# Encoder block on one core: the gated product in its own tile, partial sums in u, w_down's work tied to rounds, two score units in the projection

## The chip, the core and the metric

The kernel runs on one core of a Trainium2 chip, as one program with one launch. The metric is the device time of that core in microseconds (us). Five engines work side by side, each through its own queue in order: PE (TensorE, matmuls and transposes; its weight loads are listed as PEld), DVE (VectorE), ACT (ScalarE), POOL (GpSimd) and SP (SyncE, which here only issues DMAs). They meet through semaphores. The profile also gives the clock that TensorE was granted, as a share of 2.4 GHz.

## What is computed

One layer of a bidirectional encoder over 1024 tokens of width 1024, in float32:

```python
h = rmsnorm(x, norm_mix_pre)                      # 1. token mixing
y = parallel_mixer(h, ...)                        #    conv group and 8-head attention, one projection in, one out
x = x + rmsnorm(y, norm_mix_post)
h = rmsnorm(x, norm_mem_pre)                      # 2. cross-attention into 256 memory tokens
y = memory_cross_attention(h, mem_n, ...)
x = x + rmsnorm(y, norm_mem_post)
h = rmsnorm(x, norm_ffn_pre)                      # 3. gated MLP, D_FF = 2816
u = dwconv_centred(h @ w_up, ffn_dw, ffn_dw_b)    #    width 3 over tokens
gate, val = u[..., :D_FF], u[..., D_FF:]
y = (gelu(gate, approximate=True) * val) @ w_down
x = x + rmsnorm(y, norm_ffn_post)
```

In the attention, query heads are normalised, rotated by position and multiplied with the keys; softmax runs over all 1024 keys.

## The kernel before, in words

Each float32 product is made of three matmuls (`gemm3`, `gemm3_multi`): operands are split into a rounded part and a remainder, both in float32r. The rounded part is a cast on ACT, the remainder a subtraction on DVE or POOL (`a_split`, L774 to L776).

The program order is not what runs: the Tile framework's scheduler works through the code with a time model of its own and fixes one order for each engine, and a tile from a pool is given out only when an earlier holder of a slot is done. Pools that matter here: `tmp` (4 slots of 128x1024), `raw` (3 slots of that size, where weights land), `W` (7 slots, the split operands), `A` (15 slots), and in PSUM `psB` (4 banks) and `psS` (2 pairs of banks). `tc.issue_after(ins)` puts the instructions of a block behind `ins` in the order of its engine.

**Projection and attention.** A loop of 16 steps (L504) projects keys and values of 8 token tiles, then queries of 8 tiles (`q_proj`, 24 matmuls each, with normalisation and rotation in a `tmp` tile, `qbuf`). Three steps behind, `q_transpose` turns a query tile into the operand `Q`. Tiles 5, 6 and 7 are turned inside the attention loop (L592, at u = 2, 4, 6). That loop runs over 64 units: `att_scores(u)` is four matmuls into a `psS` pair, a maximum on DVE (L539) and an exponential on ACT (L542) into a `tmp` tile `P`; three units later `att_transpose` turns P on PE and splits it, and every second unit `att_values` multiplies with V.

**The up stage of the MLP.** w_up is handled in 22 rounds of 128 gate and 128 value columns. A round uses a two-by-two scheme with seven products (Strassen's, in a form with shared sums) on halves of the inner and the token dimension. One product is 12 matmuls, so a round is 84. `up_first(fi)` makes the first two products (operands b11 and b21), `up_operands(fi)` the sums and splits of the weights (POOL L808 to L811, ACT L775, DVE L776), `up_finish(fi)` the products p6, p5, p3, p7 and p4 with operands t2, t1, b22, t3 and t4. The five operands of the tokens are made once, by `cross_operands` at t = 4 to 7; the last is t4, whose remainder is the last DVE step there (L708).

Partial sums go into a `tmp` tile `q`, results into a `W` tile `u` (gate and value). `conv3` is the width-3 convolution: an ACT step (L825) and two DVE steps (L826, L828). Then come the GELU on ACT (L854) and the gated product on DVE (L859), which writes into u's second half; a DMA stores this half to `act_d` (L860).

**w_down's sums, made beside.** The down stage needs four differences of w_down's blocks. For each of 22 slices `down_load` brings 512 KB into one of two halves of the `A` tile `wd_b`, `down_sums` makes four subtractions in place on DVE (L769), and `down_store` writes them to `T_d`. Nothing ties a slice to a round: only the two halves of wd_b and the order that the scheduler gave limit how soon they run. All loads and stores of the stage are issued by SP, in order.

**The down stage** (L890 on) reads act_d, w_down and T_d; its matmuls write `yd`. It runs seven products (m1, m2, m6, ...); T_d is first read by the third. Its activations land in `acts`, tiles from pool `A`.

Of the kernel before, what the change touches and what calls it, by code (L numbers as in the profile page):

```python
# [34 lines left out]
def encoder_block(ctx: ExitStack, tc: tile.TileContext, x, xT, mem, w_a, w_q, w_kv, w_mkv, w_mqT,  # L35
# [446 lines left out]
    def q_proj(t):  # L482
        pq = psB("pq")
        proj(pq, t, wq, 2)
        buf = bufs[8 + t] = tmp("qbuf")
        q3, rb = norm_rope(pq, 8, t, buf, gq[:, :128], 0.125)
        nc.vector.tensor_tensor(out=q3, in0=q3, in1=rb, op=ALU.mult)
# [12 lines left out]

    B_LAG = 3
    KV_LAG = 6
    nkv = [0]
    for i in range(16):  # L504
        if i < 16:
            (kv_proj if i < 8 else q_proj)(i % 8)
        if i >= 8:
            conv_stats(i - 8)
        if i == 13:
            conv_apply(0)  # L510
        upto = min(i - KV_LAG, 7) if i < 8 else min(7, 7 - KV_LAG + 2 * (i - 7))
        while nkv[0] <= upto:
            kv_transpose(nkv[0])
            nkv[0] += 1
        if i >= 8 + B_LAG:
            q_transpose(i - 8 - B_LAG)
    b_ctx.__exit__(None, None, None)
# [9 lines left out]
    def att_scores(u):  # L527
# [14 lines left out]
        return nc.scalar.activation(out=P, in_=sp, func=AF.Exp, bias=nm, accum_out=att_r[qp, i][:, hd:hd + 1])  # L542

# [60 lines left out]

# [21 lines left out]

    def load_raw(src, name):
        r = raw(name)
        nc.sync.dma_start(out=r, in_=src)
        return r  # L630
# [132 lines left out]
    def down_load(fi):  # L763
        nc.sync.dma_start(out=wd_b[:, fi % 2], in_=down_slice(w_down, fi))

    def down_sums(fi):
        b11, b12, b22, b21 = [wd_b[:, fi % 2, b, :] for b in range(4)]
        for dst, in0, in1 in ((b11, b12, b11), (b12, b22, b12), (b22, b22, b11), (b21, b22, b21)):
            nc.vector.tensor_tensor(out=dst, in0=in0, in1=in1, op=ALU.subtract)  # L769

    def down_store(fi):
        nc.sync.dma_start(out=down_slice(T_d, fi), in_=wd_b[:, fi % 2])

    def a_split(dst, src, eng):  # L774
        nc.scalar.copy(out=dst[:, 0, :], in_=src)  # L775
        eng.tensor_tensor(out=dst[:, 1, :], in0=src, in1=f(dst[:, 0, :]), op=ALU.subtract)  # L776
# [11 lines left out]
    def up_first(fi):  # L788
# [6 lines left out]
        q = tmp("q")  # L795
# [7 lines left out]
    def up_operands(fi):  # L803
# [12 lines left out]
        a_split(a3[:, 1], s34[:, H0], nc.vector)  # L816
# [3 lines left out]
        ups[fi] = (a2, a3, a22[0][:, fi % 2], u, q)  # L820

# [10 lines left out]
    def up_finish(fi):  # L832
        a2, a3, a22_, u, q = ups.pop(fi)

        def add(dst, ps, other, op=ALU.add, swap=False):
            nc.vector.tensor_tensor(out=dst, in0=other if swap else ps, in1=ps if swap else other, op=op)  # L836
# [14 lines left out]
        add(q[:, H0], p7, q[:, H0])  # L851
        add(u[:, 1, H1], p5, q[:, H0])
        cg = conv3(fi, 0, u)
# [5 lines left out]
        nc.vector.tensor_tensor(out=u[:, 1], in0=u[:, 0], in1=cv, op=ALU.mult)  # L859
        nc.sync.dma_start(out=act_d[fi], in_=u[:, 1])  # L860
# [11 lines left out]
    for fi in range(NF + 1):  # L872
        if fi < NF:
            if fi >= UP_PRE:
                up_first(fi)
            up_operands(fi)
        if fi == 0:
            down_load(0)
        else:
            down_store(fi - 1)  # L880
            up_finish(fi - 1)
        if fi < NF:
            down_sums(fi)
        if fi + 1 < NF:
            down_load(fi + 1)
# [208 lines left out]
```

## Time and profile before

| | us |
|---|---|
| median of 3 runs | 1452.29 (1451.33 to 1456.73) |
| the profiled execution, its own time | 1453.6 |
| its span, first to last instruction | 1451.5 |
| PE busy | 1383.5 (95%) |
| DVE busy | 1070.8 (74%) |
| ACT busy | 699.9 (48%) |
| POOL busy | 514.0 (35%) |

PE is busy for 95% of the span, so the time that any change can win lies mostly in the stretches where PE is idle or has a lower clock. Busy shares are averages over stages: the views by stretch say where PE waits, and the lists of waits say for whom. Of an engine that works in order, the instruction that waits need not be the one that matters; those behind it wait too.

### The profile page before, as it was taken

What the parts mean: (1) busy time and instruction counts of PE and PEld (TensorE: products, weight loads), DVE (VectorE), ACT (ScalarE), POOL (GpSimd) and SP (SyncE); (2) the same over time, 40 slices, a digit from 0 to 9 for tenths busy, and PEclk for the clock granted to TensorE, in tenths of its full rate; (3) what the DMA queues carried; (4) which work ended last, traced back from release to release, by engine and by line L of the source; (5) the groups of instructions that cost most, each with busy time, mean ns of one, the idle gap of its engine ahead of it and who ended that gap; (6) DMA issues with size and microseconds to landing.
All of it is one profiled execution on the core that took longest, in us unless ns stands there. A gap on an engine that the chain in (4) does not pass through costs nothing.

```text
span 1451.5 us, 18836 instructions
## 1 busy us (share of the span) xinstructions
PE 1383.5 (95%) x7042; PEld 1167.5 (80%) x7042; DVE 1070.8 (74%) x1442; ACT 699.9 (48%) x1191; POOL 514.0 (35%) x506
## 2 busy tenths in 40 slices
PE   9999999799999999999996989789999999999996
PEld 7889988679898888888885767678888888888885
DVE  6699899799998334335458878877777778985576
ACT  7426543588888434334444424234444443544452
POOL 5548887600102324002136525345554441000003
PEclk9999999999999999999998999899999999999998
DMA  6417750000000434013223576742222228622325
GB/s 236 135 59 238 243 200 14 19 1 2 30 1 12 163 103 151 24 43 131 87 87 102 174 232 198 236 135 83 74 93 81 88 87 317 226 88 88 109 87 210
DMA packets 74060, 170.08 MB, mean 117 GB/s; under 512 B 9713, under 2 KB 32497, under 8 KB 73969
## 3 DMA queue, kind: packets, MB, share of 16 engines
q1 hardware_dynamic: 73968, 168.88, 35.1%
q8 instruction: 55, 0.90, 0.3%
q14 instruction: 37, 0.30, 0.1%
HBM read 124.82 MB, written 44.04 MB: 116 GB/s over the span
## 4 chain that ended last, share of the span: by engine, by line
PE 62%; DVE 7%; DMA 5%; ACT 2%; issue 2%; POOL 1%; POOLq 0%; DVEq 0%; ACTq 0%; SPq 0%
PE p L98 7%; PE p L99 6%; PE p L101 6%; PE yd L91 5%; PE yd L92 5%; PE yd L93 5%; PE y L99 4%; PE y L101 4%; PE y L98 4%; PE pPT L82 3%; DVE wd L769 3%; DMA wd<-in_w_down_dram 2%; DMA T_d<-wd 2%; PE sc L101 2%; PE sc L98 2%; PE sc L99 2%
## 5 line engine op out<-in xcount | busy, mean ns | idle before, releaser
L305 DVE SCALAR_TENSOR_TENSOR cacc<-conv,col,cacc 128x1009 f32<-128x1009 f32 (+14 forms) x120 | 145.8, 1276 | 4.7 <-ACT cacc L253 4.5
L86 POOL TENSOR_SCALAR rt<-ss 128x1 f32<-128x1 f32 (+1 forms) x43 | 15.0, 349 | 353.5 <-DVE ss L920 227.2
L92 PE MATMUL yd<-op 128*128 128x512 f32 x308 | 119.8, 389 | 0.0
L93 PE MATMUL yd<-op 128*128 128x512 f32 x308 | 119.7, 389 | 0.0
L775 ACT CAST a<-s 128x512 fp32r<-128x512 f32 x88 | 50.8, 621 | 105.6 <-PE p L101 65.1
L91 PE MATMUL yd<-op 128*128 128x512 f32 x308 | 96.9, 389 | 0.0
L930 ACT CAST op<-acts 128x512 fp32r<-128x512 f32 x77 | 48.0, 624 | 99.6 <-PE yd L93 87.8
L776 POOL TENSOR_TENSOR a<-wg,a 128x512 fp32r<-128x512 f32 x44 | 63.1, 1456 | 84.1 <-ACT a L775 84.0
L920 DVE TENSOR_TENSOR op<-acts,op 128x512 fp32r<-128x512 f32 x77 | 53.1, 690 | 46.5 <-ACT op L930 46.4
L826 DVE SCALAR_TENSOR_TENSOR c<-u,col,c 128x1023 f32<-128x1023 f32 x44 | 56.6, 1285 | 39.9 <-ACT c L825 39.9
L557 DVE TENSOR_TENSOR PL<-pPT,PH 128x512 fp32r<-128x512 f32 x128 | 83.2, 681 | 2.4 <-ACT PH L556 1.4
L539 DVE TENSOR_REDUCE nm<-sp 128x1 f32<-128x1024 f32 x64 | 78.0, 1218 | 7.3 <-PE sp L537 6.8
L825 ACT ACTIVATE c<-u,col 128x1024 f32<-128x1024 f32 x44 | 53.2, 1209 | 54.8 <-DVE u L836 53.4
L542 ACT ACTIVATE P<-sp,nm 128x1024 f32<-128x1024 f32 x64 | 72.2, 1128 | 15.4 <-PE pPT L82 6.5
L776 DVE TENSOR_TENSOR a<-s,a 128x512 fp32r<-128x512 f32 x88 | 67.0, 779 | 15.2 <-ACT a L775 15.0
L556 ACT CAST PH<-pPT 128x512 fp32r<-128x512 f32 x128 | 69.4, 593 | 13.9 <-PE pPT L82 13.4
L769 DVE TENSOR_TENSOR wd<-wd 128x256 f32<-128x256 f32 x88 | 57.0, 664 | 20.5 <-DMA wd<-in_w_down_dram 20.0
L82 PE MATMUL pPT<-ident,P 128*128 128x128 f32 x512 | 67.9, 273 | 0.7 <-DVE PL L557 0.7
L92 PEld LDWEIGHTS yd<-op 128*128 128x128 f32 x308 | 57.8, 188 | 12.4 <-DVE op L920 0.4
L91 PEld LDWEIGHTS yd<-op 128*128 128x128 f32 x308 | 57.8, 188 | 12.0
L93 PEld LDWEIGHTS yd<-op 128*128 128x128 f32 x308 | 57.8, 188 | 12.0
L776 POOL TENSOR_TENSOR a<-wv,a 128x512 fp32r<-128x512 f32 x22 | 32.9, 1513 | 97.5 <-ACT a L775 83.1
(344 smaller groups left out, 4395.1 us busy)
## 6 DMA issues: line engine op xcount, KB each, us to landing
wg<-in_w_up_dram SPq DMA_DIRECT2D x22, 512.0 KB, 4.4
wv<-in_w_up_dram SPq DMA_DIRECT2D x22, 512.0 KB, 4.2
wd<-in_w_down_dram SPq DMA_DIRECT2D x22, 512.0 KB, 4.2
T_d<-wd SPq DMA_DIRECT2D x22, 512.0 KB, 3.9
act_d<-u SPq DMA_DIRECT2D x22, 512.0 KB, 2.9
acts<-act_d SPq DMA_DIRECT2D x22, 512.0 KB, 6.8
st<-T_d SPq DMA_DIRECT2D x20, 512.0 KB, 3.7
wmkv_r<-in_w_mkv_dram SPq DMA_DIRECT2D x16, 512.0 KB, 4.1
```

The costliest lines, as they stand in the source:

```text
L82: nc.tensor.transpose(out=out_, in_=in_, identity=ident)
L91: nc.tensor.matmul(out=ps, lhsT=sh, rhs=mh, start=first, stop=False)
L92: nc.tensor.matmul(out=ps, lhsT=sh, rhs=ml, start=False, stop=False)
L93: nc.tensor.matmul(out=ps, lhsT=sl, rhs=mh, start=False, stop=last)
L98: nc.tensor.matmul(out=p, lhsT=sh, rhs=mh, start=first, stop=False)
L99: nc.tensor.matmul(out=p, lhsT=sh, rhs=ml, start=False, stop=False)
L101: ins = nc.tensor.matmul(out=p, lhsT=sl, rhs=mh, start=False, stop=last)
L305: nc.vector.scalar_tensor_tensor(out=acc[:, t0:t1_], in0=a[:, t0 + o:t1_ + o], scalar=cc(C_DW + c * 31 + j), in1=acc[:, t0:t1_], op0=ALU.m ...
L539: nc.vector.reduce_max(out=nm, in_=sp, axis=AX.X, negate=True)
L557: nc.vector.tensor_tensor(out=PL[dst], in0=p3, in1=f(PH[dst]), op=ALU.subtract)
L769: nc.vector.tensor_tensor(out=dst, in0=in0, in1=in1, op=ALU.subtract)
L776: eng.tensor_tensor(out=dst[:, 1, :], in0=src, in1=f(dst[:, 0, :]), op=ALU.subtract)
```

## The change

Four things are changed, all in the order and the place of the work; the arithmetic is the same.

1. In the up stage the partial sums `q` move from a tmp tile into the second half of `u`, and the gated product goes to a tmp tile `o`, from which it is stored.
2. w_down's slices are tied to rounds: the load and the store of a slice stand behind the round's last w_up load in SP's order, the four subtractions of slice fi + 1 behind the seventh sum of round fi (slice 0: behind the last split of round 0).
3. Query tiles 5 and 6 take staging tiles (`raw`) in place of tmp tiles; tiles 5 to 7 are turned at u = 2, 3, 4.
4. The score units 0 and 1 are traced in the last two steps of the projection.

```diff
-        buf = bufs[8 + t] = tmp("qbuf")
+        buf = bufs[8 + t] = (raw if t in (5, 6) else tmp)("qbuf")
...
+    EARLY = 2
...
+        if i >= 16 - EARLY:
+            att_scores(i - 16 + EARLY)
...
-    for u in range(NU + LOOKAHEAD + 2):
-        if u < NU:
+    for u in range(EARLY, NU + LOOKAHEAD + 2):
+        if EARLY <= u < NU:
             ex = att_scores(u)
...
-        if u in (2, 4, 6):
-            q_transpose(8 - B_LAG + u // 2 - 1)
+        if u < EARLY + 3:
+            q_transpose(8 - B_LAG + u - EARLY)
...
     def load_raw(src, name):
         r = raw(name)
-        nc.sync.dma_start(out=r, in_=src)
+        last_load[0] = nc.sync.dma_start(out=r, in_=src)
...
     def down_load(fi):
-        nc.sync.dma_start(out=wd_b[:, fi % 2], in_=down_slice(w_down, fi))
-
-    def down_sums(fi):
+        with tc.issue_after(last_load[0].ins):
+            nc.sync.dma_start(out=wd_b[:, fi % 2], in_=down_slice(w_down, fi))
+
+    def down_sums(fi, behind):
...
+        with tc.issue_after(behind.ins):
+            for dst, in0, in1 in ((b11, b12, b11), (b12, b22, b12), (b22, b22, b11), (b21, b22, b21)):
+                nc.vector.tensor_tensor(out=dst, in0=in0, in1=in1, op=ALU.subtract)
...
     def down_store(fi):
-        nc.sync.dma_start(out=down_slice(T_d, fi), in_=wd_b[:, fi % 2])
+        with tc.issue_after(last_load[0].ins):
+            nc.sync.dma_start(out=down_slice(T_d, fi), in_=wd_b[:, fi % 2])
...
-        q = tmp("q")
+        q = u[:, 1, :]
...
-        add(q[:, H0], p7, q[:, H0])
+        seventh = add(q[:, H0], p7, q[:, H0])
         add(u[:, 1, H1], p5, q[:, H0])
+        if fi + 1 < NF:
+            down_sums(fi + 1, seventh)
...
-        nc.vector.tensor_tensor(out=u[:, 1], in0=u[:, 0], in1=cv, op=ALU.mult)
-        nc.sync.dma_start(out=act_d[fi], in_=u[:, 1])
+        o = tmp("o")
+        nc.vector.tensor_tensor(out=o, in0=u[:, 0], in1=cv, op=ALU.mult)
+        nc.sync.dma_start(out=act_d[fi], in_=o)
...
             if fi >= UP_PRE:
                 up_first(fi)
-            up_operands(fi)
-        if fi == 0:
-            down_load(0)
+                down_store(fi - 2)
+            lo = up_operands(fi)
+            down_load(fi)
+        if fi:
+            up_finish(fi - 1)
         else:
-            down_store(fi - 1)
-            up_finish(fi - 1)
-        if fi < NF:
-            down_sums(fi)
-        if fi + 1 < NF:
-            down_load(fi + 1)
+            down_sums(0, lo)
+    for fi in (NF - 2, NF - 1):
+        down_store(fi)
```

Three places show how the scheduler's order moves.

The first is PE near the end of the projection (pln and plnT are transposes of the conv group, pqT those of a query tile, sp a score unit); minus is before, plus is now.

```order
 L82 MATMUL plnT<-ident,n_2322 128x128 x8
 L82 MATMUL pln<-ident,conv_414 128x128
-L82 MATMUL pln<-ident,conv_413 128x128 x2
-L82 MATMUL pln<-ident,conv_414 128x128 x2
+L518 MATMUL sp<-KH,Q_1901 128x512
+L519 MATMUL sp<-KL,Q_1901 128x512
+L518 MATMUL sp<-KH,Q_1901 128x512
+L519 MATMUL sp<-KL,Q_1901 128x512
 L82 MATMUL plnT<-ident,n_2322 128x128 x4
 L82 MATMUL pqT<-ident,qbuf 128x128 x4
```

Score unit 0 now stands ahead of the last two query projections; the transposes of the last conv tile went behind them. Unit 1 still follows the projection.

The second is DVE at the start of the up stage, right behind t4's remainder (a<-s is a remainder of weight sums, wd<-wd one of w_down's subtractions, the other rows add a product p to a partial sum). Before:

```order
L708 TENSOR_TENSOR t4l<-r_b_6641,t4h 128x4x128 x4
L776 TENSOR_TENSOR a_7463<-s_7457,a_7463 128x512
L776 TENSOR_TENSOR a_7464<-s_7458,a_7464 128x512 x2
L776 TENSOR_TENSOR a_7490<-s_7484,a_7490 128x512
L769 TENSOR_TENSOR wd<-wd 128x256 x6
L836 TENSOR_TENSOR q<-p_7503,q 128x512
```

Now:

```order
L713 TENSOR_TENSOR t4l<-r_b_6641,t4h 128x4x128 x4
L784 TENSOR_TENSOR a_7487<-s_7481,a_7487 128x512 x2
L784 TENSOR_TENSOR a_7488<-s_7482,a_7488 128x512 x2
L845 TENSOR_TENSOR u<-p_7500,u 128x512
L776 TENSOR_TENSOR wd<-wd 128x256
L845 TENSOR_TENSOR u<-p_7501,u 128x512
```

Round 0's weight remainders went ahead of t4's, round 1's stand where they stood, and one w_down subtraction in place of six is between them and the second product's sum.

The third is a round, on DVE and on SP. DVE before, in round 2 (a_7782 belongs to round 3; c<-u,col,c is a step of the convolution):

```order
L769 TENSOR_TENSOR wd<-wd 128x256
L776 TENSOR_TENSOR a_7782<-s_7776,a_7782 128x512
L769 TENSOR_TENSOR wd<-wd 128x256
L776 TENSOR_TENSOR a_7782<-s_7776,a_7782 128x512
L769 TENSOR_TENSOR wd<-wd 128x256 x2
L836 TENSOR_TENSOR u<-p_7822,q 128x512
L769 TENSOR_TENSOR wd<-wd 128x256 x4
L826 SCALAR_TENSOR_TENSOR c<-u,col,c 128x1023
```

The same round now, from its third sum on:

```order
L845 TENSOR_TENSOR u<-p_7819,u 128x512
L835 SCALAR_TENSOR_TENSOR c<-u,col,c 128x1023
L845 TENSOR_TENSOR u<-p_7833,u 128x512
L776 TENSOR_TENSOR wd<-wd 128x256
L837 SCALAR_TENSOR_TENSOR c<-u,col,c 128x1023
L845 TENSOR_TENSOR u<-p_7792,u 128x512
L776 TENSOR_TENSOR wd<-wd 128x256
L845 TENSOR_TENSOR u<-u,p_7857 128x512
L776 TENSOR_TENSOR wd<-wd 128x256 x2
L835 SCALAR_TENSOR_TENSOR c<-u,col,c 128x1023
```

Eight subtractions in this stretch became four, all behind the seventh product's sum, and none stands ahead of a weight remainder. SP's queue in the same rounds before:

```order
L772 DMA T_d<-wd 512x1x256 x2
L764 DMA wd<-in_w_down_dram 128x4x256 x2
L772 DMA T_d<-wd 512x1x256
L629 DMA wv<-in_w_up_dram 128x1024
L764 DMA wd<-in_w_down_dram 128x4x256
L860 DMA act_d<-u 128x1024
L772 DMA T_d<-wd 512x1x256
L764 DMA wd<-in_w_down_dram 128x4x256
```

Now, one round's worth:

```order
L634 DMA wv<-in_w_up_dram 128x1024
L770 DMA wd<-in_w_down_dram 128x4x256
L634 DMA wg<-in_w_up_dram 128x1024
L780 DMA T_d<-wd 512x1x256
L872 DMA act_d<-o 128x1024
```

Where up to three slices a round went through, there is now one load and one store of w_down in each round, in a fixed cycle with the loads of w_up and the store of the gated product.

## Rows read from the trace of the kernel before

**Rows 1.** Busy time by engine, granted clock, DMA share, in stretches of the up stage.
```profile
core 0: us, PE busy (x) PEld busy (x) DVE busy (x) ACT busy (x) POOL busy (x), PEclk, DMA share, GB/s
757.96:798.90 40.94, 27.99 (x107) 21.81 (x106) 34.73 (x42) 21.14 (x39) 26.62 (x19) 0.83 0.28 90
...
803.67:980.00 176.33, 154.42 (x635) 122.77 (x636) 145.57 (x204) 61.76 (x86) 72.10 (x54) 0.94 0.60 194
980.00:1200.00 220.00, 220.00 (x972) 182.21 (x972) 159.67 (x186) 94.14 (x129) 108.83 (x82) 1.00 0.26 83
```

**Rows 2.** The same columns without POOL, for instructions on the products p alone.
```profile
803.67:1230.53 426.86, 404.95 (x1740) 330.06 (x1740) 98.98 (x147) 11.74 (x20) 0.98 0.45 147
```

**Rows 3.** What PE waited for most, 757 to 1231 us: total, times, longest.
```profile
PE p L98 <- ACT a L775: 21.8, 7, 5.7
```

**Rows 4.** PE in time order: start, duration, instruction, idle before and its releaser.
```profile
784.50 0.79 PE L101 MATMUL p<-t1h,a 128*128 128x512 f32 x1 [5.06 <-DVE a L776]
...
803.67 0.47 PE L98 MATMUL p<-b11h,a 128*128 128x512 f32 x1 [1.76 <-DVE u L836]
...
849.31 0.80 PE L98 MATMUL p<-b11h,a 128*128 128x512 f32 x1 [5.49 <-ACT a L775]
...
920.62 0.80 PE L98 MATMUL p<-b11h,a 128*128 128x512 f32 x1 [5.68 <-ACT a L775]
...
966.69 0.50 PE L98 MATMUL p<-b11h,a 128*128 128x512 f32 x1 [3.28 <-ACT a L775]
```

**Rows 5.** DVE and ACT ahead of the gap at 849, in time order.
```profile
844.17 0.42 DVE L769 TENSOR_TENSOR wd<-wd 128x256 f32<-128x256 f32 x1 [3.10 <-DMA wd<-in_w_down_dram]
...
847.51 1.21 ACT L825 ACTIVATE c<-u,col 128x1024 f32<-128x1024 f32 x1 [10.61 <-DVE u L836]
848.66 1.12 ACT L775 CAST a<-wg 128x512 fp32r<-128x512 f32 x2
```

**Rows 6.** ACT ahead of the gaps at 920 and 966, in time order.
```profile
917.78 1.14 ACT L775 CAST a<-wv 128x512 fp32r<-128x512 f32 x2 [10.79 <-DMA act_d<-u]
...
963.85 1.14 ACT L775 CAST a<-wv 128x512 fp32r<-128x512 f32 x2 [7.36 <-DMA act_d<-u]
```

**Rows 7.** w_down's subtractions: ns min/median/max; then busy us, mean ns, idle before.
```profile
L769 DVE TENSOR_TENSOR wd<-wd x88: 403/419/1515, 792.8 to 954.1; 128x256 f32<-128x256 f32 x88
...
L769 DVE TENSOR_TENSOR wd<-wd 128x256 f32<-128x256 f32 x88 | 57.0, 664 | 20.5 <-DMA wd<-in_w_down_dram 20.0
```

**Rows 8.** What DVE waited for most in the rounds without w_down, 980 to 1200 us.
```profile
DVE c L826 <- ACT c L825: 29.4, 23, 1.3
```

**Rows 9.** Start of the up stage in time order: DVE, SP, DVE, POOL.
```profile
784.37 2.48 DVE L708 TENSOR_TENSOR t4l<-r_b,t4h 128x512 fp32r<-128x512 f32 x4
...
786.92 1.34 SPq L764 DMA_DIRECT2D wd<-in_w_down_dram  x2
...
792.78 5.37 DVE L769 TENSOR_TENSOR wd<-wd 128x256 f32<-128x256 f32 x6
...
789.77 1.29 POOL L808 TENSOR_TENSOR s<-wv 128x512 f32<-128x512 f32 x1
```

**Rows 10.** The columns of Rows 1 around the start of the attention.
```profile
255.00:276.00 21.00, 19.54 (x97) 15.79 (x96) 12.37 (x21) 11.38 (x19) 17.40 (x27) 0.92 0.11 32
276.00:304.00 28.00, 18.26 (x107) 13.91 (x106) 26.98 (x37) 20.64 (x37) 6.39 (x10) 1.00 0.00 1
```

**Rows 11.** PE and ACT at the start of the attention.
```profile
280.36 0.50 PE L536 MATMUL sp<-KH,Q 128*128 128x512 f32 x1 [3.19 <-ACT P L542]
...
277.81 1.28 ACT L542 ACT_TABLE_LOAD   x1
```

**Rows 12.** The columns of Rows 1 where the down stage begins; SP's loads there.
```profile
1220.00:1240.00 20.00, 20.00 (x90) 16.57 (x89) 19.93 (x28) 8.76 (x12) 0.00 (x0) 1.00 0.99 372
1240.00:1260.00 20.00, 20.00 (x90) 16.54 (x90) 20.00 (x34) 10.33 (x20) 0.00 (x0) 1.00 0.72 242
...
1201.03 0.81 SPq L895 DMA_DIRECT2D acts<-act_d  x2
```

More of the change, by code (lines that the diff above doesn't have):

```diff
@@ L499, in q_transpose @@
             nc.vector.tensor_tensor(out=Q[h][e][hi, :, ts_], in0=pt3[lo], in1=f(Q[h][e][lo, :, ts_]), op=ALU.subtract)
[L501 to L517, printed above, removed]
     NU = 64
@@ L542, in att_scores @@
         return nc.scalar.activation(out=P, in_=sp, func=AF.Exp, bias=nm, accum_out=att_r[qp, i][:, hd:hd + 1])
+    B_LAG = 3
+    EARLY = 2
+    KV_LAG = 6
+    nkv = [0]
+    for i in range(16):
+        if i < 16:
+            (kv_proj if i < 8 else q_proj)(i % 8)
+        if i >= 8:
+            conv_stats(i - 8)
+        if i == 13:
+            conv_apply(0)
+        upto = min(i - KV_LAG, 7) if i < 8 else min(7, 7 - KV_LAG + 2 * (i - 7))
+        while nkv[0] <= upto:
+            kv_transpose(nkv[0])
+            nkv[0] += 1
+        if i >= 8 + B_LAG:
+            q_transpose(i - 8 - B_LAG)
+        if i >= 16 - EARLY:
+            att_scores(i - 16 + EARLY)
+    b_ctx.__exit__(None, None, None)
     def att_transpose(u):
@@ L625, in post_norm @@
         return t
+    last_load = [None]
     def load_raw(src, name):
         r = raw(name)
-        nc.sync.dma_start(out=r, in_=src)
+        last_load[0] = nc.sync.dma_start(out=r, in_=src)
         return r
@@ L763, in down_load @@
     def down_load(fi):
-        nc.sync.dma_start(out=wd_b[:, fi % 2], in_=down_slice(w_down, fi))
-    def down_sums(fi):
+        with tc.issue_after(last_load[0].ins):
+            nc.sync.dma_start(out=wd_b[:, fi % 2], in_=down_slice(w_down, fi))
+    def down_sums(fi, behind):
         b11, b12, b22, b21 = [wd_b[:, fi % 2, b, :] for b in range(4)]
-        for dst, in0, in1 in ((b11, b12, b11), (b12, b22, b12), (b22, b22, b11), (b21, b22, b21)):
-            nc.vector.tensor_tensor(out=dst, in0=in0, in1=in1, op=ALU.subtract)
+        with tc.issue_after(behind.ins):
+            for dst, in0, in1 in ((b11, b12, b11), (b12, b22, b12), (b22, b22, b11), (b21, b22, b21)):
+                nc.vector.tensor_tensor(out=dst, in0=in0, in1=in1, op=ALU.subtract)
     def down_store(fi):
-        nc.sync.dma_start(out=down_slice(T_d, fi), in_=wd_b[:, fi % 2])
+        with tc.issue_after(last_load[0].ins):
+            nc.sync.dma_start(out=down_slice(T_d, fi), in_=wd_b[:, fi % 2])
     def a_split(dst, src, eng):
         nc.scalar.copy(out=dst[:, 0, :], in_=src)
-        eng.tensor_tensor(out=dst[:, 1, :], in0=src, in1=f(dst[:, 0, :]), op=ALU.subtract)
+        return eng.tensor_tensor(out=dst[:, 1, :], in0=src, in1=f(dst[:, 0, :]), op=ALU.subtract)
     def product(ps, a, b):
@@ L815, in up_operands @@
         a_split(a3[:, 0], s34[:, H1], nc.vector)
-        a_split(a3[:, 1], s34[:, H0], nc.vector)
+        lo = a_split(a3[:, 1], s34[:, H0], nc.vector)
         if fi % 2 == 0:
@@ L820, in up_operands @@
         ups[fi] = (a2, a3, a22[0][:, fi % 2], u, q)
+        return lo
     def conv3(fi, gv, u):
@@ L835, in add @@
         def add(dst, ps, other, op=ALU.add, swap=False):
-            nc.vector.tensor_tensor(out=dst, in0=other if swap else ps, in1=ps if swap else other, op=op)
+            return nc.vector.tensor_tensor(out=dst, in0=other if swap else ps, in1=ps if swap else other, op=op)
         p6, p5 = psB("p6"), psB("p5")
```

## The prediction, before the changed kernel ran

> **What bounds the kernel now.** The reading begins with the busy shares: PE 95%, the next engine 74%. So the question is where PE loses its 5% and what clock it has. The view by stretches answers for the up stage [rows 1]. From 980 to 1200 us PE is busy for all of 220.00 us at clock 1.00 and starts 972 matmuls: 0.2263 us each, 19.0 us for a round of 84. From 803.67 to 980 it has 21.9 us of idle time and a mean clock of 0.94, and from 757.96 to 798.90 it is idle for 13.0 us at 0.83. From the first product of round 2 to the first matmul of the down stage 426.86 us pass, with 1740 product matmuls [rows 2]; at 0.2263 they would need 393.8. So **33.0 us** are lost there, all of it before 980. 21.9 are idle time; the other 11 are the lower clock: 0.94 over 176.33 us means that some 21 us ran at 1.2 GHz, which costs half of that.
>
> The list of waits names ACT's casts of weights first, 21.8 us [rows 3], and PE in time order gives the gaps: 5.49, 5.68 and 3.28 us, each ahead of a b11 product, whose operand is a cast of wg [rows 4]. Followed back, they have two causes. At 849 DVE stood for 3.10 us before a w_down subtraction whose load had not landed; weight remainders and product sums were queued behind it, ACT waited 10.61 us for one of these sums to begin the convolution, and the cast of wg stood behind that [rows 5]. At 920 and 966 ACT stood 10.79 and 7.36 us at a cast into a W slot that the store of u's second half still held [rows 6]; the convolution and the cast of wg were behind it. The first cause is what the change ties to rounds, the second what it takes out with the tile o. From 980 on w_down's work is over (the last subtraction starts at 954.1 [rows 7]), stores of u go on, and PE loses nothing.
>
> **A. The rounds.** The ties leave one load and one store of 512 KB and four subtractions in each round, the latter behind the seventh sum. Their load is issued a round ahead, so DVE should not stand before it. u's slot is free when the product is done, and not when the store has landed. What is new is DVE's load in the rounds that ran full before. There DVE was busy 159.67 of 220 us [rows 1]: 13.8 us a round, idle 5.2. The subtractions bring 57.0 us over 22 rounds [rows 7], 2.6 a round, so that 2.6 of idle time stay. Not all of it can be used: 29.4 us in 11.6 rounds, 2.5 each, are DVE waiting for ACT's step of the convolution [rows 8]. But in the order two of the four subtractions stand just in one of these gaps (between the last sum and the second convolution), worth 1.3. So a round needs 13.8 + 2.6 + 1.3 = 17.7 of 19.0: it fits, with 1.3 to spare. SP's queue in a round is w_up value, w_down load, w_up gate, T_d store, act_d store. The T_d store waits for the subtractions, the act_d store for the product; behind them wait the weight loads for three and four rounds later, which have more than a round of time. The tmp tile o is held by a store, again for less than a round. I take 3 us of leftover stalls while the pipeline fills, 0 to 10 as bounds (one gap as those at 849 and 920 with its slow clock is 8 to 10): **−30 us**, between −33 and −23.
>
> **B. The start of the stage.** Before, PE stood 5.06 us in the first t1 product for a weight remainder and reached round 2 at 803.67 [rows 4]. With q in tmp, two of four slots were held and round 1's sums on POOL began at 789.77, when round 0's were read; then six subtractions took DVE for 5.37 us from 792.78, ahead of the first sum [rows 9]. Now round 0's remainders stand ahead of t4's and no slot is missing. What stays: t4's remainder ends at 786.85, and only then can w_down's load be issued (786.92, the A tile is free no earlier [rows 9]). It reached DVE by 792.78, and in the new order one subtraction stands between the sums of the first and the second product. So DVE can pass at about 792.5; two sums and a second subtraction later (0.7, 0.4, 0.7) a bank is free, and round 2 begins at about 795: **−8.5 us**. If POOL's sums for round 1 come as late as before, their remainders hold the same sum until about 801: −2. If the load lands at once, the limit is t4's own product, 790.5: −13.
>
> **C. The attention's start.** From 276 to 304 PE is idle 9.7 of 28 us, but DVE is busy for 26.98 [rows 10]; the wait for a free P slot at 280.36 [rows 11] is thus only partly worth something, and freeing tmp slots (3) helps only until DVE is the limit. Of DVE's work one maximum, about 1.2 us, moves ahead, and the statistics of the last conv tile, about 0.9, come in. The moved score unit fills a gap in a stretch whose clock was 0.92 over 21 us [rows 10], 3.4 us at half clock, 1.7 lost. The load of the exponential's table, 1.28 us on ACT at 277.81 [rows 11], lies in the projection now; I count 0.5 of it. 1.7 + 0.3 + 0.5: **−2.5 us**. Bounds: +1 if the score unit only delays the projections (four matmuls, 0.9), −6 if most of PE's idle time there goes.
>
> **D. The change of stages.** Here the change costs. DVE is full from 1220 to 1260 and the DMA engines too [rows 12]. Before, w_down's work was long over; now the last four subtractions (2.6 us) and two stores (1 MB, 3 us at 372 GB/s) fall into it, and the slot of wd_b, which held the first act_d load early, frees last, so the loads that began at 1201.03 become one tile more. DVE's combinations of acts stand in its queue ahead of the last sums and would wait for these loads. About 5.5 us of extra DMA time, part of it hidden by the 29 us between the loads' begin and the first yd: **+3.5 us**, 0 to +9.
>
> **Sum.** −30 − 8.5 − 2.5 + 3.5 = −37.5 us. Against the profiled execution, 1453.6 (span 1451.5), that is 1416; against the median of the runs, 1452.3, it is **1415**. The bounds add to −52 and −15: 1400 and 1437.
>
> **Rivals.**
> *DVE becomes the bound in every round.* For it: only 1.3 us are spare, and one subtraction took up to 1515 ns where the median is 419 [rows 7]. At 1.3 us each, a round needs 13.8 + 1.3 + 5.2 = 20.3; 1.3 over, 26 us in 20 rounds: 1441. Against it: the mean of 664 ns comes from a stretch where POOL was busy for 72.10 of 176.33 us, and it is 108.83 of 220 in the full rounds [rows 1], hardly more.
> *The same, slower than before.* If each subtraction waits for a whole POOL instruction (1.29 us [rows 9]) it takes 1.7 us, a round 21.9, and 20 rounds lose 58: 1473. It ends above the old time once the mean passes about 1.45 us. The Trainium skill, page "SBUF — State Buffer", section "Who interferes with whom", has the rule behind this: a DVE instruction with two SBUF inputs and a GpSimd instruction that reads SBUF take a shared port, and the later one blocks fully. The spread from 403 to 1515 ns agrees with it; taken for each subtraction it gives the 1473.
> *The stall only changes its place.* The a22 cast, the convolution and the cast of wg stay in one ACT queue; if another wait (a weight load behind SP's two waiting stores) takes the place of those removed, half of A is left: 1430.
> *The ties do nothing.* Against it: the order shows them in each round. What could still keep the old time is A and B lost together: 1453.
>
> **How the numbers follow.** The forecast, 1400 to 1430: 0.70. Stall moved, 1428 to 1440: 0.10. DVE the bound, 1432 to 1445: 0.11. No change: 0.04. Slower by DVE: 0.05. About 0.5% (7 us) is what a measurement of this kernel can tell from no change; so faster by more than that 0.91, within 0.04, slower 0.05. The range 1401 to 1438 takes in the forecast with its bounds, the moved stall and half of the DVE case; some 0.15 is left out.
>
> **What would show it.** Right: the stretch from the first product to the first yd falls from 472.6 us to about 434; no b11 product with an idle gap over 2 us after the third round; w_down's subtractions evenly over the stage with no DMA wait before them; DVE about 86% busy in the full rounds. B: round 2 begins some 37 us after the first product, not 46. C: the first unit's exponential ahead of the last query projection. D: some PE waits at the first yd products. Wrong: PE gaps before p products in every round whose releaser is a DVE sum (first rival), a mean subtraction over 1 us, or casts that wait for wv or wg loads.

## The result: half of the gain went to the change of stages

The changed kernel takes **1436.8 us** (median of 4 runs, 1436.0 to 1438.7); the kernel before takes 1454.5 in the runs beside it. The ratio is 0.988, with a 95% interval from 0.9855 to 0.9905: 17.7 us faster, less than half of the 37.5 that were forecast. The profiled execution has a span of 1436.9 us, 14.6 less than the 1451.5 of before.

Cut at the points that the prediction named, the two profiled executions compare so (us; "round 2" is its first b11 product, yd the products of the down stage):

| stretch | term | before | after | difference | forecast |
|---|---|---|---|---|---|
| start to first product | C | 758.0 | 758.7 | +0.7 | -2.5 |
| first product to round 2 | B | 45.7 | 45.6 | -0.1 | -8.5 |
| round 2 to first yd | A | 426.9 | 394.7 | -32.1 | -30 |
| first yd to last yd | D | 209.5 | 226.0 | +16.5 | +3.5 |
| last yd to end | D | 11.4 | 11.8 | +0.4 | (in D) |

Over the whole span the shares moved little; the page of after has, busy us by engine (share of the span):

```profile
PE 1380.9 (96%) x7042; PEld 1167.6 (81%) x7042; DVE 1102.4 (77%) x1442; ACT 699.4 (49%) x1191; POOL 529.5 (37%) x506
```

The stretches tell more: the main term came as forecast, the start of the up stage gave nothing, and the change of stages took back half. The same columns as in [rows 1], for the two stretches of the up stage of after:

```profile
core 0: us, PE busy (x) PEld busy (x) DVE busy (x) ACT busy (x) POOL busy (x), PEclk, DMA share, GB/s
758.68:804.31 45.63, 31.18 (x119) 23.52 (x118) 42.72 (x43) 21.00 (x40) 32.24 (x23) 0.85 0.30 92
...
804.31:1199.03 394.72, 394.72 (x1741) 326.52 (x1741) 356.48 (x429) 166.61 (x228) 195.99 (x136) 1.00 0.46 155
```

Against [rows 2] PE has no idle time left from round 2 to the first yd, and its granted clock is 1.00: 394.72 us for the same products, 0.9 above the 393.8 that they need. None of the gaps of [rows 4] behind round 2 is left. In the first stretch DVE is busy for 42.72 of 45.63 us, so it is taken for the limit there; the run b_dve tests this. The longest of PE's waits from the first product on, in total, times, longest:

```profile
PE yd L91 <- ACT op L941: 5.6, 1, 5.6
PE yd L91 <- DVE u L845: 5.6, 2, 3.1
PE p L99 <- DVE t3l L713: 3.9, 1, 3.9
```

The first two rows are the change of stages. In stretches of it (the columns above), after:

```profile
1190.00:1200.00 10.00, 10.00 (x46) 8.15 (x45) 10.00 (x18) 5.36 (x7) 0.00 (x0) 1.00 0.96 376
1200.00:1210.00 10.00, 4.52 (x15) 2.51 (x13) 10.00 (x15) 2.16 (x3) 0.00 (x0) 0.81 1.04 403
1210.00:1220.00 10.00, 4.24 (x9) 2.94 (x10) 9.93 (x15) 5.46 (x9) 0.00 (x0) 0.50 0.72 237
1220.00:1230.00 10.00, 10.00 (x39) 8.03 (x39) 5.74 (x10) 3.21 (x7) 0.00 (x0) 0.84 0.81 272
```

Before, PE was full here while DVE and the DMA engines were full too [rows 12]. Now PE stands in three gaps (start, duration, instruction, idle time before it and its releaser):

```profile
1205.39 0.50 PE L91 MATMUL yd<-op 128*128 128x512 f32 x1 [3.07 <-DVE u L845]
...
1210.19 0.80 PE L91 MATMUL yd<-op 128*128 128x512 f32 x1 [2.49 <-DVE u L845]
...
1218.69 2.07 PE L91 MATMUL yd<-op 128*128 128x512 f32 x4 [5.57 <-ACT op L941]
```

That is 11.1 us of idle time. The granted clock is 0.50 from 1208 to 1222 and 1.00 again from 1224 on; most of the other 5.4 of the 16.5 us are matmuls that ran at 1.2 GHz.

Behind the first two gaps stand PSUM banks: the third and fourth token tiles of yd need banks that the last product sums of the up stage have not read yet, and on DVE these sums stand behind combinations of acts, which belong to the down stage (L931):

```profile
1203.45 0.68 DVE L931 TENSOR_TENSOR op<-acts,op 128x512 fp32r<-128x512 f32 x1
1204.06 0.68 DVE L931 TENSOR_TENSOR acts<-acts 128x512 f32<-128x512 f32 x1
1204.66 0.68 DVE L845 TENSOR_TENSOR u<-p,u 128x512 f32<-128x512 f32 x1
1205.26 1.28 DVE L931 TENSOR_TENSOR acts<-acts 128x512 f32<-128x512 f32 x2
...
1209.46 0.68 DVE L845 TENSOR_TENSOR u<-u,p 128x512 f32<-128x512 f32 x1
```

In DVE's order 20 instructions of the down stage and 4 subtractions of w_down stand between the first sum of round 20 and the last sum of round 21; before it was 14 and none. The last sum starts 10.4 us after the first yd, before 2.6 us. Behind the third gap stands SP's queue:

```profile
1177.36 1.95 SPq L924 DMA_DIRECT2D st<-in_w_down_dram  x2
...
1203.56 0.32 SPq L872 DMA_DIRECT2D act_d<-o  x1
1212.14 0.32 SPq L908 DMA_DIRECT2D acts<-act_d  x1
1212.51 2.97 SPq L924 DMA_DIRECT2D st<-in_w_down_dram  x4
```

st is a pair of weight slices of w_down. At 1212.14 SP issues a load of acts that had to wait for the store of the gated product of round 20, and four loads of st stood behind it. Their casts are the first that PE misses. In the kernel before, a first load at 1192.41 and the following four were out by 1211.5, 19 us ahead of the first yd:

```profile
1192.41 0.38 SPq L913 DMA_DIRECT2D st<-in_w_down_dram  x1
...
1202.96 0.57 SPq L913 DMA_DIRECT2D st<-in_w_down_dram  x1
...
1207.36 4.18 SPq L913 DMA_DIRECT2D st<-in_w_down_dram  x3
```

### The profile page after: what moved, and what is told of

Same layout as the page of the kernel before. It is cut to its first block, busy times and chain, and to the rows that moved or that the text cites. A ratio compares the mean times of both kernels' runs of the same rounds, so it can differ in the third digit from the quotient of the medians.

```text
span 1436.9 us, 18839 instructions
## 1 busy us (share of the span) xinstructions
PE 1380.9 (96%) x7042; PEld 1167.6 (81%) x7042; DVE 1102.4 (77%) x1442; ACT 699.4 (49%) x1191; POOL 529.5 (37%) x506
## 4 chain that ended last, share of the span: by engine, by line
PE 81%; DVE 9%; POOL 4%; issue 3%; ACT 2%; DMA 1%; SPq 0%; POOLq 0%; DVEq 0%; ACTq 0%
PE p L98 8%; PE p L101 8%; PE p L99 8%; PE yd L91 5%; PE yd L92 5%; PE yd L93 5%; PE y L99 4%; PE y L101 4%; PE y L98 4%; PE pPT L82 3%; PE sc L101 2%; PE sc L98 2%; PE sc L99 2%; PE sp L518 2%; PE po L570 2%
## 5 line engine op out<-in xcount | busy, mean ns | idle before, releaser
L92 PE MATMUL yd<-op 128*128 128x512 f32 x308 | 121.3, 394 | 0.0
L93 PE MATMUL yd<-op 128*128 128x512 f32 x308 | 121.2, 394 | 0.0
L91 PE MATMUL yd<-op 128*128 128x512 f32 x308 | 102.8, 396 | 11.2 <-ACT op L941 5.6
L931 DVE TENSOR_TENSOR op<-acts,op 128x512 fp32r<-128x512 f32 x77 | 53.0, 688 | 55.5 <-ACT op L941 55.4
L784 POOL TENSOR_TENSOR a<-wg,a 128x512 fp32r<-128x512 f32 x44 | 68.5, 1579 | 60.4 <-ACT a L783 60.4
L784 DVE TENSOR_TENSOR a<-s,a 128x512 fp32r<-128x512 f32 x88 | 89.7, 1058 | 0.0
L524 ACT ACTIVATE P<-sp,nm 128x1024 f32<-128x1024 f32 x64 | 72.2, 1127 | 14.6 <-PE pPT L82 8.0
L845 DVE TENSOR_TENSOR u<-p,u 128x512 f32<-128x512 f32 x110 | 75.0, 683 | 5.5 <-PE p L101 4.6
```

Source lines behind the costliest of these rows:

```text
L91: nc.tensor.matmul(out=ps, lhsT=sh, rhs=mh, start=first, stop=False)
L92: nc.tensor.matmul(out=ps, lhsT=sh, rhs=ml, start=False, stop=False)
L93: nc.tensor.matmul(out=ps, lhsT=sl, rhs=mh, start=False, stop=last)
L784: return eng.tensor_tensor(out=dst[:, 1, :], in0=src, in1=f(dst[:, 0, :]), op=ALU.subtract)
L845: return nc.vector.tensor_tensor(out=dst, in0=other if swap else ps, in1=ps if swap else other, op=op)
```

## Experiments

All runs at a glance: stretches of the profiled run (us) and the median of the timed runs. Each ratio is to runs of the kernel before that were taken beside that kernel's; their medians are 1454.5 for after, 1454.4 for the next four kernels, 1453.4 for st_raw to ties_only, and 1452.5 for the last four, so medians of different groups compare to about 2 us.

| kernel | first product to round 2 | round 2 to first yd | first to last yd | median | ratio to before, 95% |
|---|---|---|---|---|---|
| before | 45.7 | 426.9 | 209.5 | 1454.5 | |
| after | 45.6 | 394.7 | 226.0 | 1436.8 | 0.9855 to 0.9905 |
| d_both | 44.5 | 394.6 | 222.0 | 1431.8 | 0.9830 to 0.9859 |
| d_dve | 45.4 | 394.7 | 222.3 | 1433.8 | 0.9842 to 0.9878 |
| d_sp | 44.3 | 394.8 | 225.6 | 1436.9 | 0.9865 to 0.9898 |
| no_late | 45.5 | 396.4 | 224.7 | 1439.0 | 0.9882 to 0.9912 |
| st_raw | 44.4 | 395.5 | 220.9 | 1430.8 | 0.9829 to 0.9859 |
| st_dve | 44.5 | 394.6 | 211.3 | 1421.1 | 0.9765 to 0.9796 |
| before_o | 46.7 | 418.7 | 224.7 | 1462.5 | 1.0046 to 1.0080 |
| ties_only | 45.0 | 416.9 | 211.4 | 1445.1 | 0.9927 to 0.9957 |
| c_off | 44.4 | 395.5 | 211.6 | 1424.3 | 0.9787 to 0.9814 |
| b_dve | 42.4 | 395.0 | 211.8 | 1419.0 | 0.9754 to 0.9781 |
| o_twice | 46.5 | 406.0 | 211.6 | 1435.3 | 0.9867 to 0.9895 |
| o_three | 45.3 | 415.9 | 214.0 | 1446.0 | 0.9942 to 0.9967 |

### The change of stages: a first theory that fell

The first theory took the two queues at their word: DVE's and SP's order in the change of stages. Its rival was the prediction's own reason for term D, w_down's late work. d_both alters both orders, d_dve and d_sp one each, and no_late leaves w_down's late work out.

```diff
+            with tc.issue_after(m1_low[min(i + 6, NH - 1)].ins):      # d_dve, d_both
-            comb(V_, a21, a21, a22, ALU.add)
-            comb(V_, a11, a21, a11)
-            comb(V_, a12, a12, a11)
+                comb(V_, a21, a21, a22, ALU.add)
+                comb(V_, a11, a21, a11)
+                comb(V_, a12, a12, a11)
```

m1_low[k] is DVE's second remainder of operand k of the first product. For SP:

```diff
-    for i in range(NH):                                               # d_sp, d_both
+    def acts_right(i):
         nc.sync.dma_start(out=acts[i][:, 2:4, :], in_=act_d[i + NH]...)
...
+    for i in range(NH - 2):
+        acts_right(i)
...
         t_ = right(name, i)
+        if name == "m1" and i == NH - 1:
+            for j in (NH - 2, NH - 1):
+                acts_right(j)
```

d_both:

> The changed kernel with two orders altered in the change of stages: on DVE the combinations of acts that w_down's second product needs are put behind the remainders of its first product, and on SP the loads of the last two right halves of acts are put behind the weight loads (st) of the first product. Theory (the loss at the change of stages is the order of these two queues): the two waits of PE for a DVE sum (3.07 and 2.49 us) and the wait for a cast (5.57 us) go, and with them the lower clock behind them; from the first to the last yd product 209 to 212 us instead of 225.6, time about 1421. Rival (w_down's last subtractions and stores and the late slot of wd_b, as the prediction had it in its term D): the queues' order matters little, the stretch stays above 220, time 1432 to 1437.

d_dve:

> Only the DVE half of d_both. Theory: the two waits for a DVE sum at the first yd products go (5.6 us and some 3 us of lower clock), the wait of 5.57 us for a cast of a weight whose load stands behind a waiting acts load on SP stays or shrinks only as far as the product of round 20 comes earlier: stretch 215 to 219 us, time 1427 to 1431. Rival (w_down's last work): as for d_both, above 220.

d_sp:

> Only the SP half of d_both. Theory: the wait of 5.57 us goes, the two waits for DVE sums stay: stretch 216 to 220 us, time 1428 to 1432. If instead the casts wait for DVE and not for the load, nothing changes: 225, 1437.

Measured: 222.0, 222.3 and 225.6 us from first to last yd. The theory expected 209 to 212, 215 to 219 and 216 to 220; all three lie where the rivals had them (above 220, and 225 for d_sp). The two waits for DVE sums are gone in d_both and d_dve, so their cause was rightly named, but the third wait grew. PE of d_both:

```profile
1211.73 2.07 PE L91 MATMUL yd<-op 128*128 128x512 f32 x4 [9.61 <-ACT op L949]
```

And ACT:

```profile
1211.06 1.14 ACT L949 CAST op<-st 128x512 fp32r<-128x512 f32 x2 [4.02 <-DMA st<-in_w_down_dram]
```

In d_both the load of acts that waits for a store no longer stands ahead of st in SP's queue; the late loads of st are issued from 1200.74 on, and still the cast waits for its data until 1211.06. So SP's order was not the whole cause: these loads come too late even at 1200, behind the loads of acts (22 of 512 KB) that fill the DMA engines. Which leaves the question why they were not issued at 1177, with the other two.

> The changed kernel without w_down's work for the last two rounds: no load, no subtractions, no store there; two plain copies from w_down to T_d in round 12 stand in, so the last two slices of T_d hold the raw weights and the output is not the reference's. The slot of wd_b comes free two rounds earlier. Rival (the prediction's term D: 2.6 us of subtractions, 3 us of stores, one slot late): the first yd product finds its operands as early as before, stretch about 210 to 213 us, time 1421 to 1425. Theory (queue orders): only the four subtractions of 1.7 us in all that stand ahead of the last sums go, and the loads begin earlier without the order being changed: stretch 220 to 225 us, time 1431 to 1437.

Measured: 224.7 us, 1439.0. Without w_down's late subtractions, loads and stores nearly all of the loss stays: the stretch is 1.3 us shorter than the 226.0 of after, and the time no better. The reason that the prediction gave for term D does not carry the loss. Since the other waits could have hidden it here, ties_only below, which keeps the late work and loses less than 2 us, is the stronger test.

### The staging slots

st alternates between raw and tmp, two pools of staging tiles. The order of SP's queue in the changed kernel, with tile numbers, shows which st is late: 10623, 10695 and 10767 (operands 0 and 1, 4 and 5, 8 and 9, all in raw) go ahead of the acts, while

```
283 L924 DMA st_10832<-in_w_down_dram 128x2x512 [waits DMAHW2_49,DVE_49]
284 L906 DMA acts_10602<-act_d_6642 128x1024 [waits DMAHW3_49,PE_49]
285 L910 DMA gF_10615<-in_rows_dram 128x1024 [waits DMAHW4_49,PE_49]
286 L872 DMA act_d_6642<-o_10494 128x1024 [waits DMAHW5_49,DVE_49]
287 L908 DMA acts_10600<-act_d_6642 128x1024 [waits DMAHW6_49,DMAHW5_49]
288 L924 DMA st_10659<-in_w_down_dram 128x2x512 [waits DMAHW7_49]
289 L924 DMA st_10731<-in_w_down_dram 128x2x512 [waits DMAHW0_49]
```

10659 (operands 2 and 3) and 10731 (6 and 7), in tmp, stand behind the product of round 20; even st_10832, which belongs to the second product, goes ahead of them. tmp has four slots, and at the end of the up stage s12 and s34 of the last round and the new tile o of the last two rounds ask for them. Before, the product had no tile in tmp, and both loads were issued from 1207.36 on. Who holds a slot is not in the trace, but the built program tells more: 10659 takes a slot that s34 of the last round had, whose last reader on DVE ended at 1182.34; yet 10659, 10731 and the load behind them (10803, operand 10) stand directly behind the instruction that writes o of the last round. So o need not hold the slot that st takes; it is enough that it stands ahead of st in the line for slots. That this costs the time is a theory to be tested, S: the new tile took the staging slots of the next stage's weights, or their turn. Two tests: other slots for st, and each half of the change alone on the kernel before.

```diff
-            st = (tmp if nst[0] % 2 == 0 else raw)("st")...                                  # st_raw, st_dve
+            st = (raw if nst[0] <= 3 else tmp if nst[0] <= 6 or nst[0] % 2 == 0 else raw)("st")...
```

> The changed kernel, and only the staging slots of w_down's weights in its first product altered: the first three loads (st) take the three raw slots and the next three tmp slots, instead of raw and tmp in turn. Theory S (tmp slots: o of the last rounds holds them, so the weights for the operands 2 and 3 are loaded only after the product of round 20 and behind 11 MB of acts): PE's wait for a cast of st, 5.57 us, falls below 1.5 us; the two waits for DVE sums, 5.6 us, stay; from the first to the last yd product about 217 us instead of 226, time about 1429. Rival (the DMA engines are full from 1185 to 1211 us and any such load lands late): the wait stays at 5 us or more, 225, 1436.

> st_raw and d_dve together. Theory S with the order of DVE's queue: no wait of PE over 1.5 us behind the first yd product, from the first to the last yd product 209 to 212 us as in the kernel before, time 1419 to 1422. Rival (full DMA engines): a wait of 5 to 10 us for a cast stays as in d_dve, 1432.

Measured: 1430.8 and **1421.1**, 220.9 and 211.3 us from first to last yd. In st_raw the wait for a cast of st is gone and DVE's queue is what is left; it costs more than the theory expected (a stretch of about 217 us, a time of about 1429):

```profile
PE yd L92 <- DVE op L931: 4.0, 1, 4.0
...
PE yd L91 <- DVE u L845: 2.1, 1, 2.1
```

With both edits the largest wait in the down stage is

```profile
PE yd L91 <- ACT op L943: 1.3, 1, 1.3
```

and the stretch is within 1.8 us of before, though the DMA engines are as full as ever (0.97 from 1180 to 1200 and 1.00 from 1200 to 1220). The rival of full DMA engines falls with it. Neither edit alone does this: d_dve with the old slots gives 222.3, st_raw with the old order 220.9.

The halves of the change on the kernel before:

```diff
-        q = tmp("q")                                                                         # before_o
+        q = u[:, 1, :]
...
-        nc.vector.tensor_tensor(out=u[:, 1], in0=u[:, 0], in1=cv, op=ALU.mult)
-        nc.sync.dma_start(out=act_d[fi], in_=u[:, 1])
+        o = tmp("o")
+        nc.vector.tensor_tensor(out=o, in0=u[:, 0], in1=cv, op=ALU.mult)
+        nc.sync.dma_start(out=act_d[fi], in_=o)
```

ties_only is the changed kernel with these lines, and the parts of the change in the projection, as before.

> The kernel before with the tile o for the product and the partial sums in u's second half, and nothing else of the change. Prediction's reading of term A: the gaps of 5.68 and 3.28 us at 920 and 966 (a cast waiting for u's slot) go, the gap of 5.49 us at 849 (a subtraction of w_down waiting for its load) stays; from the first product of round 2 to the first yd 405 to 412 us instead of 426.9. Theory S: o is in tmp here too, so the change of stages loses as in the changed kernel, from the first to the last yd product 218 to 228 us; if it is w_down's late work that loses there, 209 to 212. Time 1440 to 1450.

> Only the ties of w_down's work to rounds: the product in place, the partial sums in tmp, no early score units, query tiles as before. Prediction's reading of term A: the gap at 849 goes, casts waiting for u's slot stay in the rounds while the pipeline fills; from the first product of round 2 to the first yd 403 to 415 us. Theory S: no tile o in tmp, so from the first to the last yd product 209 to 213 us although w_down's work now lies at the end of the stage; if w_down's late work is the cause, 220 or more. Time 1430 to 1445.

Measured: before_o **1462.5**, 0.6% slower than before where 1440 to 1450 was expected, with 224.7 us from first to last yd and the same kinds of wait as after:

```profile
PE yd L91 <- ACT op L931: 6.9, 1, 6.9
PE yd L91 <- DVE u L836: 4.4, 2, 3.7
```

ties_only has 211.4 us there, with w_down's work in the last rounds and the DMA engines at 1.01 and 1.03:

```profile
1200.00:1220.00 20.00, 20.00 (x90) 16.57 (x89) 17.96 (x28) 6.70 (x9) 0.00 (x0) 1.00 1.01 381
1220.00:1240.00 20.00, 19.05 (x82) 14.80 (x81) 20.00 (x30) 10.63 (x17) 0.00 (x0) 1.00 1.03 407
```

So the loss comes with the first part of the change, which brings o (and takes q out of tmp), and not with the ties; with st_raw, in which other slots alone end the wait for st, theory S holds. The same two kernels take term A apart. From round 2 to the first yd before_o has 418.7 us and ties_only 416.9, where 405 to 412 and 403 to 415 were expected and both together give 394.7. Each half leaves the other cause in place: in before_o DVE still waits for w_down's loads, and in ties_only ACT's casts wait for u's slot (total, times, longest from 804 to 1190):

```profile
DVE wd L769 <- DMA wd<-in_w_down_dram: 16.0, 11, 2.8
```

```profile
ACT a L783 <- DMA act_d<-u: 86.4, 19, 6.0
```

Alone they are worth 8 and 10 us, together 32. Where the rest is lost shows in PE's idle time. In before_o its 14.1 us in these rounds all lie before 980, as the 21.9 do in the kernel before. In ties_only there are 7.9 us from 980 to 1190, where the kernel before had none:

```profile
980.00:1190.00 210.00, 202.09 (x868) 164.05 (x867) 161.36 (x206) 81.48 (x115) 94.98 (x72) 0.98 0.41 131
```

So the ties alone carry w_down's work into the rounds that ran full, and there it meets the casts that wait for u's slot.

### DVE's margin in a round

The forecast had 1.3 us of DVE to spare in a round, and its first rival none. To measure it the gated product is written twice or three times over, on st_dve:

```diff
+        nc.vector.tensor_tensor(out=o, in0=u[:, 0], in1=cv, op=ALU.mult)      # once: o_twice, twice: o_three
         nc.sync.dma_start(out=act_d[fi], in_=o)
```

> The kernel st_dve with the gated product written twice in every round: 1.21 us more of DVE a round. DVE is busy 161.98 of 180 us in the full rounds, 17.1 of 19.0 a round, and 1.6 us more is its waiting for ACT's step of the convolution. If only the busy time counts, 18.3 of 19.0 still fits and the time stays within 3 us of 1421. If the waits for ACT can't be filled, 19.9 is 0.9 too much in some 20 rounds: about 1439.

> The same with the gated product written three times: 2.42 us more of DVE a round, 19.5 of 19.0 us by the busy time alone: 0.5 too much in 20 rounds is 10 us, 1431. With the waits for ACT 21.1, 2.1 too much: 42 us, 1463. Either way DVE has become the bound of every round, as the prediction's first rival had it.

Measured: 1435.3 and 1446.0, so 14 and 25 us more. Two rows of the full rounds, o_twice:

```profile
980.00:1160.00 180.00, 176.03 (x769) 143.43 (x768) 162.52 (x192) 70.02 (x99) 91.74 (x67) 1.00 0.39 132
```

and o_three:

```profile
980.00:1160.00 180.00, 173.91 (x747) 139.82 (x746) 172.27 (x197) 69.96 (x99) 91.20 (x64) 0.99 0.40 136
```

PE has idle time at once. DVE is busy 90% in o_twice, no more than without the extra work, because the rounds became longer: busy time alone did not decide. The expectation from busy plus waiting time (1439) is nearer for one product more, and for two it is too high (1463), since there DVE's waits for ACT shrink from 16.7 us in this stretch to 6.0. One more DVE instruction of 1.2 us a round costs 11 of the 32 us that term A brings (406.0 against 394.6 from round 2 to the first yd), and 14 in the whole time.

### The start of the up stage

```diff
+        eng = nc.vector if fi == 1 else nc.gpsimd                             # b_dve, on st_dve
-        nc.gpsimd.tensor_tensor(out=s12[:, H0], in0=rv[:, H0], in1=rv[:, H1], op=ALU.add)
+        eng.tensor_tensor(out=s12[:, H0], in0=rv[:, H0], in1=rv[:, H1], op=ALU.add)
...                                                                           (all four sums)
```

> The kernel st_dve with round 1's four sums of w_up on DVE instead of POOL. Theory P (at the start of the up stage DVE is the limit because its two-input instructions take 1.4 to 1.76 us while POOL works on round 1's sums, and 0.68 us when it does not): the four remainders t3l take under 3.5 us instead of 5.72, the four sums add 2.8 us on DVE, and round 2 begins 40 to 43 us after the first product instead of about 44 to 45; time 1417 to 1420. Rival (the start hangs on PE's and ACT's own order of t1 to t4, or on DVE's amount of work): no change or up to 3 us slower.

Measured: round 2 begins 42.4 us after the first product instead of 44.5, and the time is 1419.0. The stretch moved as theory P expected, by 2.1 us; the medians differ by 2.1 too, but their intervals overlap. The mechanism shows in the durations. In after, DVE beside POOL's sums of round 1 (784 to 792 us):

```profile
783.83 5.73 DVE L713 TENSOR_TENSOR t3l<-r_b,t3h 128x512 fp32r<-128x512 f32 x4
789.48 1.77 DVE L716 TENSOR_TENSOR r_b<-r_b,r_b 128x512 f32<-128x512 f32 x1
791.17 1.77 DVE L784 TENSOR_TENSOR a<-s,a 128x512 fp32r<-128x512 f32 x1
```

The same instructions in b_dve:

```profile
781.04 3.56 DVE L713 TENSOR_TENSOR t3l<-r_b,t3h 128x512 fp32r<-128x512 f32 x4
784.53 0.68 DVE L716 TENSOR_TENSOR r_b<-r_b,r_b 128x512 f32<-128x512 f32 x1
785.13 0.68 DVE L784 TENSOR_TENSOR a<-s,a 128x512 fp32r<-128x512 f32 x1
```

### The attention's start

c_off is st_dve with EARLY = 0, all query tiles in tmp, and the last query tiles transposed behind units 2, 4 and 6.

> The kernel st_dve without the attention part of the change (no score units in the projection, all query tiles in tmp). The prediction's term C says that this part is worth 2.5 us (between +1 and -6): 1423.5. The first trace of the changed kernel says that it is worth about nothing (the up stage's first product at 758.7 against 758.0): 1420 to 1422.

Measured: 1424.3 against 1421.1, with intervals that overlap a little. The up stage's first product comes at 756.5, 758.0, 760.9 and 761.6 us in the four traces without this part, 759.2 on the mean, and at 756.1 to 759.8 in the ten with it, 757.7 on the mean. Both differences, 1.5 and 3.2 us, have the sign and about the size of the forecast, but neither is clear of the spread, and the +0.7 of the two first traces lies within it too. That the part is worth 1.5 to 3 us is likely and not shown.

## Why the prediction was half right

The measured 1436.8 lies in the stated range of 1401 to 1438 and in the ranges of two rivals (the stall that changes its place, 1428 to 1440, and DVE as the bound, 1432 to 1445). That is luck: neither of the two took place in the rounds, where term A came in full. Two other terms failed, B and D.

**A, -30, measured -32.1.** Both causes were right: before_o and ties_only each still show the one that they leave in place. But their effects do not add up (8, 10, together 32), and the margin beside it was thin. DVE in the full rounds (980 to 1160 us, x is the count, then busy us and mean ns), after:

```profile
L784 DVE TENSOR_TENSOR a<-s,a 128x512 fp32r<-128x512 f32 x40 | 42.1, 1093 | 0.0
...
L776 DVE TENSOR_TENSOR wd<-wd 128x256 f32<-128x256 f32 x37 | 26.1, 705 | 0.3
```

The subtractions cost 0.705 us as forecast (0.664 [rows 7]), not the 1.7 of the slow rival; but the weight remainders beside POOL rose from 854 ns to 1093, about 1 us a round that the sum did not have. DVE is busy 162.1 of 180 us there, 17.1 a round, and waits 1.6 for ACT: 18.7 of 19.0, where the prediction had 17.7. The first rival's condition was thus nearer than the prediction took it to be, and o_twice shows what lay behind the edge.

**B, -8.5, measured -0.1.** The step that failed is "What stays: t4's remainder ends at 786.85". It ended at 796.15:

```profile
780.83 1.28 DVE L784 TENSOR_TENSOR a<-s,a 128x512 fp32r<-128x512 f32 x2
...
793.65 2.50 DVE L713 TENSOR_TENSOR t4l<-r_b,t4h 128x512 fp32r<-128x512 f32 x4
```

The change itself moved this end. Round 0's weight remainders now stand ahead of t4's, as the prediction says in the sentence before: four of them in after, where one stood in the kernel before, and it gave them no price. And that "no slot is missing" has a cost. The freed slots let POOL begin round 1's sums at 784.10 instead of 789.77 [rows 9], into DVE's remainders t3l, of which one took 1.49 us on the mean instead of 1.19 before. w_down's first load, which was issued right behind t4's remainder before, is so again, at 796.22 instead of 786.92, and round 2 begins as late as it did. What was won in slots was lost on DVE, which is busy for 42.72 of 45.63 us there. b_dve gets 2 to 3 us of it back. What the rest of the 8.5 would need was not tried.

The Trainium skill, page "SBUF — State Buffer", section "Who interferes with whom", has the rule that a DVE instruction with two SBUF inputs contends with a GpSimd instruction that reads SBUF, one of them waiting for the other. Here 0.68 us became 1.75 beside POOL, and POOL's sums 1.71 instead of 1.27: the trace agrees that they hold each other up, and the rule was more to the point for this term than for the rival to which the prediction put it.

**C, -2.5, measured +0.7 in the first trace; 1.5 and 3.2 us gained by the fourteen traces and by c_off, neither clear of the spread.** The order came as announced: the first exponential starts at 266.52, the last query projection at 269.61. But the clock, which was 1.7 us of the term, did not simply rise. In all ten traces with this part it is 1.00 from 245 to 276 us and 0.76 to 0.94 from 276 to 304; of the four without, before and c_off have 0.94 and then 1.00, before_o and ties_only 1.00 and then 0.88. The term is not refuted, and its size is not shown.

**D, +3.5, measured +16.9.** Here lies the error that decided. The step that failed is one clause in A: "The tmp tile o is held by a store, again for less than a round." That is true in a round. But after the last round the same pool stages w_down's weights, and their loads, given out behind the last o, were issued 35 us later than their neighbours. The prediction costed the slot of wd_b, the last subtractions and 1 MB of stores, none of which is the cause by no_late and ties_only. What mattered was the tile pool that the new tile shares. "DVE's combinations of acts stand in its queue ahead of the last sums" was seen, but within a term of 3.5 us that counted DMA time: together with the staging slots it makes 11.1 us of gaps, and most of another 5.4 us are the lower clock behind them. st_dve undoes the two together and is back at 211.3 us.

Of the signs announced, the rounds without gaps, w_down's even work and the early exponential came true; the stretch from the first product to the first yd was to be about 434 us and was 440.3; DVE was to be 86% busy in the full rounds and was 90%; round 2 at 37 us did not come. "Some PE waits at the first yd products" came, but the change of stages cost 16.9 us and not 3.5.

**A version that beats both.** st_dve takes 1421.1 us (0.9765 to 0.9796 of before), b_dve 1419.0 (0.9754 to 0.9781): the change with its term D repaired, by other slots for st and another place for DVE's combinations. The span of st_dve is 32.7 us shorter than that of before; most of what it lacks of the 37.5 is term B.

## To carry to other kernels

A new tile in a shared pool must be followed to the end of its stage and beyond it: ask which tiles take slots of this pool next, and whether their loads were early only because a slot was free. A wait that goes from one queue may be covered by a second one right behind it; undo both together before a theory is dropped, as d_dve (222.3), st_raw (220.9) and st_dve (211.3) show. Count the margin of an engine with its waits for others, not by its busy time alone.

## What the runs showed of the hardware

A DVE sum of two SBUF operands of 128x512 takes 0.68 us alone and up to 1.77 beside POOL, and POOL's own sums go from 1.27 to 1.71. With four more instructions a round on DVE its old remainders beside POOL also took 28% longer on the mean (1093 ns instead of 854), which no count of instructions foretells; in o_twice, with a fifth, they took 909 and w_down's subtractions 840 instead of 705, so which of them pays depends on the order. And full DMA engines are no loss by themselves: from 1200 to 1240 us ties_only has the DMA engines at 1.01 and 1.03 and PE busy for 39 of 40 us, while in after, at 1.04 and 0.72 from 1200 to 1220, PE stands for 11 us: half of it behind DVE's order, half because weights were issued 35 us later than their neighbours.
